# Feed-forward of two superblocks by Strassen's seven products, with the weight-block sums made in the first superblock

## The chip, the cores and the metric

The kernel runs on one core of one Trainium2 chip. Its time is device microseconds of one execution; the figures below are medians over runs. The engines are TensorE (PE, with its weight load PEld), VectorE (DVE), ScalarE (ACT), GpSimd (POOL) and SyncE (SP), whose queue issues all DMA transfers here.

## The reference

One decoder layer for 2048 prompt tokens and 64 sample tokens (8 sequences of 8), model width 1024, all in float32. In order: an RMS norm and one input projection into q, k, v and u; sliding-window attention and a pooling mixer; an output projection; cross-attention into 256 memory tokens; then the feed-forward that this case is about; then a final RMS norm.

```python
    x = x + o @ w_co
    h = _rmsnorm(x, g_ffn)
    x = x + jnp.square(jax.nn.relu(h @ w_up)) @ w_down
```

`w_up` is 1024 by 4096 and `w_down` 4096 by 1024.

## The kernel before

Tokens lie on the free axis, channels on the 128 partitions. The 2112 tokens go through the layer in three superblocks of two blocks each: 384 + 384, 384 + 384, and 256 + 320 (the last block carries the 64 sample tokens). `superblock(s, blks, nxt)` runs the stages of one superblock: input projection mixed with window attention, output projection (`wo`), cross-attention (folded weights `A` and `B`), feed-forward. A residual x of 8 chunks of 128 channels lies in `XT[b]`, one tile for a block.

Every float32 operand of a matmul is held as a rounded part and a remainder (`hi`, `lo`), and each product is three matmuls: hi by hi, hi by lo, lo by hi (`mm3` at L108, `dense` at L267). Weights come as a stream: `Stream.emit` (L125) loads a 128 by 1024 block by DMA into one of six staging buffers `FS`, ACT rounds it into `th` (L132), DVE subtracts into `tl` (L133). There are twelve such buffers `WS`, so six pairs; `Stream.next` (L143) hands out the next pair in a fixed order and `pump` (L137) starts the loads that free buffers allow, at most five ahead. During window attention four of the twelve hold the keys (`kz`).

The feed-forward goes over eight groups of 512 hidden channels. `up(g)` (L1130) takes four weight blocks; for each and for both blocks of tokens it adds 24 matmuls into one PSUM bank, and `up_evac` (L1114) evicts it: ACT relu (L1122), GpSimd square (L1123), ACT rounding (L1125), DVE remainder (L1126). `down(g)` (L1135) takes four weight blocks; each gives two output chunks of 12 matmuls a block, which DVE adds to x (L1156). The order is up(0), up(1), down(0), up(2), down(1) and so on; ahead of down(6) and down(7) `norm1` begins the next superblock's first norm from a fresh load of x. Four PSUM banks (`MM`) rotate here, four more (`AUX`) serve the other stages. `Norm` (L184) squares on ACT, adds on GpSimd (L206), sums over partitions by a matmul with ones (L214) and takes the power by Ln and Exp on ACT; `apply` (L226) scales on DVE (L232), rounds on ACT (L233) and subtracts on DVE and GpSimd in turn (L235). Functions put into `later` run a few steps on, piece by piece, at each `flush` (L301), so that a norm's work stands between the matmuls of other chunks; `order` (L258) puts block 0's last three chunks ahead of block 1's, so that block 0's norm runs while block 1 is still being multiplied. Dependencies and semaphores come from the tile framework, which also sets the order of each engine's queue.

## Time and profile before

| what | value |
|---|---|
| runs | 2638.93, 2640.9, 2646.47 us; median 2640.9 |
| span of the profiled execution, first to last instruction | 2639.7 us (its time as a whole is not given apart) |
| busy PE, PEld | 2565.7 us (97%), 2458.0 us (93%) |
| busy DVE, ACT, POOL | 1302.4 us (49%), 984.2 us (37%), 680.7 us (26%) |
| DMA | 244.76 MB, mean 93 GB/s |
| mean granted TensorE clock | 0.992 |

The busy share is an average over all stages. Matmuls are pipelined, so the duration of one (some 0.33 us at 384 columns) is longer than the distance between the starts of two. An arrow in a row names what ended the idle time ahead of the instruction.

### The profile page before, as it was taken

The numbers are of one execution on the slowest core, as the hardware profiler recorded it, in microseconds if no ns is written. First come the engines' busy times: TensorE is split into PE (matmuls) and PEld (weight loads), VectorE is DVE, ScalarE is ACT, GpSimd is POOL, SyncE is SP. The second block draws the span as 40 slices with busy tenths as digits, with TensorE's granted clock in tenths as the row PEclk, the third lists the DMA queues.
The fourth block names the chain that finished last, engine by engine and source line by source line (L and its number), as shares of the span: only waits on it lengthen the run. The fifth ranks groups of instructions, "written<-read, shape, count | busy, mean of one in ns | idle before, by whom it ended". The sixth has DMA issues, their size and how long they took to land. (4 is left out here: it accounts for less than half of the span.)

```text
span 2639.7 us, 39195 instructions
## 1 busy us (share of the span) xinstructions
PE 2565.7 (97%) x15725; PEld 2458.0 (93%) x15725; DVE 1302.4 (49%) x2276; ACT 984.2 (37%) x1923; POOL 680.7 (26%) x730
## 2 busy tenths in 40 slices
PE   7899999999999999999999999999999999999998
PEld 7798979999999999997999999999999669999998
DVE  7568453633333357936363333334766646334334
ACT  6666342422222244834342222223355434332231
POOL 3215322411111153433241111113334214111111
PEclk9999999999999999999999999999999999999999
DMA  7843212211111123131111111112414473222210
GB/s 261 260 130 101 72 49 74 71 64 63 61 62 64 56 72 113 45 132 56 65 58 63 65 64 64 65 56 71 140 60 149 176 266 112 87 80 81 88 57 37
DMA packets 92251, 244.76 MB, mean 93 GB/s; under 512 B 16740, under 2 KB 31524, under 8 KB 90916
## 3 DMA queue, kind: packets, MB, share of 16 engines
q1 hardware_dynamic: 92068, 242.25, 26.9%
q8 instruction: 123, 2.02, 0.3%
q14 instruction: 60, 0.49, 0.1%
HBM read 219.53 MB, written 22.69 MB: 92 GB/s over the span
## 5 line engine op out<-in xcount | busy, mean ns | idle before, releaser
L281 PE MATMUL mm<-act,w 128*128 128x384 f32 (+2 forms) x2784 | 899.1, 323 | 6.5 <-DVE act L235 5.0
L280 PE MATMUL mm<-act,w 128*128 128x384 f32 (+2 forms) x2784 | 902.8, 324 | 2.5 <-ACT act L623 1.6
L282 PE MATMUL mm<-act,w 128*128 128x384 f32 (+2 forms) x2784 | 897.4, 322 | 1.1 <-DVE w L133 0.9
L132 ACT CAST w<-f 128x1024 fp32r<-128x1024 f32 x330 | 346.9, 1052 | 737.4 <-PE mm L112 453.9
L133 DVE TENSOR_TENSOR w<-f,w 128x1024 fp32r<-128x1024 f32 x330 | 422.8, 1286 | 317.9 <-ACT w L132 312.0
L111 PE MATMUL mm<-act,w 128*128 128x384 f32 (+2 forms) x1728 | 554.1, 321 | 13.6 <-ACT act L372 8.3
L112 PE MATMUL mm<-act,w 128*128 128x384 f32 (+2 forms) x1728 | 550.3, 318 | 0.0
L113 PE MATMUL mm<-act,w 128*128 128x384 f32 (+2 forms) x1728 | 549.8, 318 | 0.0
L281 PEld LDWEIGHTS mm<-act,w 128*128 128x128 f32 x2784 | 527.3, 189 | 16.3 <-DVE act L235 6.7
L280 PEld LDWEIGHTS mm<-act,w 128*128 128x128 f32 x2784 | 527.4, 189 | 7.2 <-issue 2.3
L282 PEld LDWEIGHTS mm<-act,w 128*128 128x128 f32 x2784 | 527.3, 189 | 1.8 <-DVE w L133 1.6
L1123 POOL TENSOR_TENSOR t<-t 128x384 f32<-128x384 f32 (+2 forms) x192 | 219.0, 1141 | 1034.8 <-ACT t L1122 1034.8
L1156 DVE TENSOR_TENSOR x<-mm,x 128x384 f32<-128x384 f32 (+2 forms) x384 | 199.7, 523 | 326.5 <-PE mm L113 326.5
L111 PEld LDWEIGHTS mm<-act,w 128*128 128x128 f32 x1728 | 328.6, 190 | 15.8 <-ACT act L372 8.3
L112 PEld LDWEIGHTS mm<-act,w 128*128 128x128 f32 x1728 | 328.3, 190 | 1.2 <-DVE act L373 0.2
L113 PEld LDWEIGHTS mm<-act,w 128*128 128x128 f32 x1728 | 328.4, 190 | 0.1
L206 POOL TENSOR_TENSOR t<-t,t 128x384 f32<-128x384 f32 (+2 forms) x168 | 203.0, 1209 | 348.9 <-ACT t L205 331.4
L1126 DVE TENSOR_TENSOR act<-t,act 128x384 fp32r<-128x384 f32 (+2 forms) x192 | 103.2, 537 | 300.4 <-ACT act L1125 300.4
L1125 ACT CAST act<-t 128x384 fp32r<-128x384 f32 (+2 forms) x192 | 93.8, 488 | 237.5 <-POOL t L1123 237.5
L1122 ACT ACTIVATE t<-mm 128x384 f32<-128x384 f32 (+2 forms) x192 | 88.2, 459 | 95.2 <-PE mm L282 94.2
L205 ACT ACTIVATE t<-x 128x384 f32<-128x384 f32 (+2 forms) x140 | 68.4, 499 | 145.4 <-DVE x L1085 64.9
L111 PE MATMUL mm<-w,act 128*128 128x512 f32 x288 | 116.7, 406 | 3.2 <-ACT f L330 1.7
(184 smaller groups left out, 2199.0 us busy)
## 6 DMA issues: line engine op xcount, KB each, us to landing
f<-in_wup SPq DMA_DIRECT2D x96, 512.0 KB, 3.5
f<-in_wdn SPq DMA_DIRECT2D x96, 512.0 KB, 3.5
f<-in_win SPq DMA_DIRECT2D x30, 512.0 KB, 3.6
f<-a_s SPq DMA_DIRECT2D x24, 512.0 KB, 3.2
f<-b_s SPq DMA_DIRECT2D x24, 512.0 KB, 4.2
x<-in_x SPq DMA_DIRECT2D x6, 1536.0 KB, 7.1
f<-in_wco SPq DMA_DIRECT2D x16, 512.0 KB, 4.9
f<-in_cmk SPq DMA_DIRECT2D x16, 512.0 KB, 4.5
```

The lines of the kernel that those rows point to most:

```text
L111: nc.tensor.matmul(ps, Wh(k), Hh(k), start=first and i == 0, stop=False)
L112: nc.tensor.matmul(ps, Wh(k), Hl(k), start=False, stop=False)
L113: nc.tensor.matmul(ps, Wl(k), Hh(k), start=False, stop=final and i == last)
L132: nc.scalar.copy(th[:], r[:, 0:1024])
L133: eng.tensor_tensor(tl[:], r[:, 0:1024], f32(th[:]), ALU.subtract)
L206: nc.gpsimd.tensor_tensor(self.acc[:, 0:n], self.acc[:, 0:n], t[:, 0:n], ALU.add)
L280: nc.tensor.matmul(ps[:, 0:n], w8(th)[:, k, :], hi(b, k), start=k == 0, stop=False)
L281: nc.tensor.matmul(ps[:, 0:n], w8(th)[:, k, :], lo(b, k), start=False, stop=False)
L282: nc.tensor.matmul(ps[:, 0:n], w8(tl)[:, k, :], hi(b, k), start=False, stop=k == 7)
L1123: nc.gpsimd.tensor_tensor(q[:, 0:n], r[:, 0:n], r[:, 0:n], ALU.mult)
L1126: nc.vector.tensor_tensor(lo, q[:, 0:n], f32(hi), ALU.subtract)
L1156: nc.vector.tensor_tensor(bl.x(m), ps[:, 0:n], bl.x(m), ALU.add)
```

## The change

The feed-forward of superblocks two and three is written anew; the first keeps the plain form.

- Tokens are cut into two halves of 384 or 288 (`nh`), and channels and hidden channels into two parts, which makes 2 by 2 blocks. `ups(g)` does seven products of 4 contraction chunks for two pairs of hidden chunks; `uevac` puts the outputs together from PSUM, applies relu and square on ACT and keeps the hidden values in float32 in `FB`. `downs(g)` does seven products of 2 contraction chunks for four pairs of output chunks and adds each into an accumulator: four of the seven live in x's own place, two (`MC`) apart, and product 1 goes into two of them. `merge` combines the six accumulators once, ahead of the last down group, which stays plain.
- The input's sums and their splits are made once (`half_ready`) and kept in 14 of the 16 `ACTS` tiles. The hidden values' sums are made on GpSimd and split for each product (`hsplit`), two products ahead, in the two other tiles.
- The sums of weight blocks are made in the first superblock's feed-forward (`prep_steps`): 60 jobs, one every second eviction step, each of which loads a block, makes five sums on DVE and stores six blocks into DRAM scratch. The plain blocks and a copy of the input projection and of the last down group go there too, copied within DRAM. Each of the seven blocks of a group is then one load of 128 by 1024.
- Weights from DRAM scratch are loaded straight into `tl` and split in place; those from the kernel's inputs still go through `FS`. `WS` has ten buffers instead of twelve, the scratch tiles `TS` six instead of eight; `FS` is cut from two large tiles `FB`, of which the feed-forward takes both; the keys `kz` have a tile of their own.
- x lies by chunk rather than by block: each of the two `XT` tiles holds four chunks for all tokens of the superblock.

```diff
+ST0 = [0, 768, 1536]
+STN = [768, 768, 576]
+WIX = {1: 0, 7: 1, 6: 2, 4: 3, 2: 4, 5: 5, 3: 6}
+ORD = (2, 4, 5, 3, 1, 7, 6)
...
-def tile_hybrid_step_kernel(ctx: ExitStack, tc: tile.TileContext, io, nW=12, nF=6, nT=8):
+def tile_hybrid_step_kernel(ctx: ExitStack, tc: tile.TileContext, io, nW=10, nT=6):
...
-    FS = Slots([sb(f"f{i}", 1088) for i in range(nF)])
+    FB = [sb(f"fb{i}", 3072) for i in range(2)]
+    FH = [[FB[h][:, 1024 * i:1024 * i + 1024] for i in range(3)] for h in range(2)]
+    FS = Slots(FH[1] + FH[0])
+    CP = [sb(f"cp{i}", 512) for i in range(2)]
...
+    win_s = drp.tile([10, P, 1024], F32, name="win_s", tag="win_s")
+    us_s = drp.tile([8, 7, P, 1024], F32, name="us_s", tag="us_s")
+    ds_s = drp.tile([7, 7, P, 1024], F32, name="ds_s", tag="ds_s")
+    dn_s = drp.tile([4, P, 1024], F32, name="dn_s", tag="dn_s")
...
         def emit(self):
-            key, raw, eng = self.items.popleft()
+            key, raw, eng, ext = self.items.popleft()
             th, tl = WS.get(), WS.get()
-            r = FS.get()
+            r = FS.get() if ext else f32(tl[:])
...
             eng.tensor_tensor(tl[:], r[:, 0:1024], f32(th[:]), ALU.subtract)
-            FS.put(r)
+            if ext:
+                FS.put(r)
             self.ready.append((key, th, tl))
...
+                for i in ORD:
+                    if g < 8:
+                        S.add(("us", s, g, i), us_s[g, WIX[i]])
+                for i in ORD:
+                    if 0 < g < 8:
+                        S.add(("ds", s, g - 1, i), ds_s[g - 1, WIX[i]], eng=nc.gpsimd if i in (5, 1) else None)
+                if g == 8:
+                    for c in range(4):
+                        S.add(("dn", s, 7, c), dn_s[c])
...
-        kz = [[WS.get() for _ in range(2)] for _ in range(2)]
+        kzt = mc_tile(F32R)
+        kz = [[kzt[:, 896 * (2 * kv + hl):896 * (2 * kv + hl) + 896] for hl in range(2)] for kv in range(2)]
...
+        def split(i, src):
+            hi, lo = ACTS.get(), ACTS.get()
+            Xc[i] = (hi, lo)
+            for j in range(2):
+                c = slice(2 * nh * j, 2 * nh * j + 2 * nh)
+                nc.scalar.copy(hi[:, c], src[:, c])
+                nc.vector.tensor_tensor(lo[:, c], src[:, c], f32(hi[:, c]), ALU.subtract)
+        def comb(dst, other, op, eng=None):
...
+        def half_ready(h):
+            X11, X21, X12, X22 = hx[0, 0], hx[1, 0], hx[0, 1], hx[1, 1]
+            if h == 0:
+                split(2, X11)
+                yield
+                comb(X21, X11, ALU.subtract)
+                split(4, X21)
+                yield
+            else:
+                split(5, X22)
+                yield
+                comb(X12, X22, ALU.subtract)
+                split(3, X12)
+                yield
+                comb(X11, X22, ALU.add)
+                split(1, X11)
+                yield
+                comb(X21, X11, ALU.add)
+                split(7, X21)
+                yield
+                comb(X12, X11, ALU.add)
+                split(6, X12)
+                yield
+                for j in range(2):
+                    x4 = XT[j][:, 0:4 * T].rearrange("p (a m t) -> p a m t", a=2, m=2)
+                    v = x4[:, :, 1, nh:2 * nh]
+                    nc.gpsimd.tensor_tensor(v, v, x4[:, :, 1, 0:nh], ALU.add)
+                    nc.gpsimd.tensor_tensor(v, v, x4[:, :, 0, nh:2 * nh], ALU.subtract)
...
+            yield
+            if blks[0].n == nh:
+                yield from half_ready(b)
+            elif b == 1:
+                yield from half_ready(0)
+                yield from half_ready(1)
...
+        def uevac(g, i, q, ps):
+            p = ps[:, 0:nh]
+            c11, c12, c21, c22 = R(g, 0, 2 * q), R(g, 1, 2 * q), R(g, 0, 2 * q + 1), R(g, 1, 2 * q + 1)
+            def relu2(v):
+                nc.scalar.activation(v, v, AF.Relu)
+                nc.scalar.activation(v, v, AF.Square)
+            if i in (2, 5):
+                t = hold[i, q] = TS.get()
+                nc.scalar.copy(t[:, 0:nh], p)
+            if i == 4:
+                nc.vector.tensor_tensor(c21, p, hold[2, q][:, 0:nh], ALU.add)
+                hold[4, q] = ps
+                relu2(c21)
+                return
+            if i == 5:
+                p4 = hold.pop((4, q))
+                nc.vector.tensor_tensor(c11, p4[:, 0:nh], hold[5, q][:, 0:nh], ALU.subtract)
+                unbank(p4)
+            if i == 3:
+                t2, t5 = hold.pop((2, q)), hold.pop((5, q))
+                nc.vector.tensor_tensor(c12, p, t5[:, 0:nh], ALU.add)
+                nc.vector.tensor_tensor(c22, p, t2[:, 0:nh], ALU.subtract)
+                TS.put(t2, t5)
+                relu2(c12)
...
+        def ups(g):
+            for i in ORD:
+                th, tl = S.next(("us", s, g, i))
+                while i not in Xc:
+                    flush()
+                Hh, Hl = Xc[i]
+                for q in range(2):
+                    ps = bank()
+                    mm3(ps[:, 0:nh], range(4), lambda k: th[:, 512 * q + P * k:512 * q + P * k + P], lambda k: tl[:, 512 * q + P * k:512 * q + P * k + P],
+                        lambda k: Hh[:, nh * k:nh * k + nh], lambda k: Hl[:, nh * k:nh * k + nh])
+                    uevac(g, i, q, ps)
+                    flush()
+                WS.put(th, tl)
...
+        def macc(i, p):
+            if i in (4, 5):
+                return MC[i - 4][:, p * nh:p * nh + nh]
+            m, h = {7: (0, 0), 3: (0, 1), 2: (1, 0), 6: (1, 1)}[i]
+            return xrow(s, 2 * p + m, h * nh, h * nh + nh)
...
+        def hsplit(g, i, dst):
+            X11, X21, X12, X22 = R(g, 0, 0, 2), R(g, 0, 2, 2), R(g, 1, 0, 2), R(g, 1, 2, 2)
+            pre = {4: (X21, X11, ALU.subtract), 3: (X12, X22, ALU.subtract), 1: (X11, X22, ALU.add),
+                   7: (X21, X11, ALU.add), 6: (X12, X11, ALU.add)}.get(i)
+            if pre:
+                nc.gpsimd.tensor_tensor(pre[0], pre[0], pre[1], pre[2])
+            src = {2: X11, 5: X22, 4: X21, 3: X12, 1: X11, 7: X21, 6: X12}[i]
+            hi, lo = dst[:, 0:2 * nh], dst[:, 2 * nh:4 * nh]
+            nc.scalar.copy(hi, src)
+            nc.vector.tensor_tensor(lo, src, f32(hi), ALU.subtract)
+            return hi, lo
+        def downs(g, after=None):
+            hc = {}
+            LEAD = len(HC)
+            def make(j):
+                if j < 7:
+                    hc[j] = hsplit(g, ORD[j], HC[j % LEAD])
+                if j == 6 and after is not None:
+                    after()
+            for j in range(LEAD):
+                make(j)
+            for j, i in enumerate(ORD):
+                th, tl = S.next(("ds", s, g, i))
+                Hh, Hl = hc[j]
+                for p in range(4):
+                    ps = bank()
+                    mm3(ps[:, 0:nh], range(2), lambda k: th[:, 256 * p + P * k:256 * p + P * k + P], lambda k: tl[:, 256 * p + P * k:256 * p + P * k + P],
+                        lambda k: Hh[:, nh * k:nh * k + nh], lambda k: Hl[:, nh * k:nh * k + nh])
+                    v = ps[:, 0:nh]
+                    if i == 1:
+                        nc.vector.tensor_tensor(macc(7, p), v, macc(7, p), ALU.add)
+                        nc.vector.tensor_tensor(macc(6, p), v, macc(6, p), ALU.add)
+                    elif g == 0 and i in (4, 5):
+                        nc.scalar.copy(macc(i, p), v)
+                    else:
+                        nc.vector.tensor_tensor(macc(i, p), v, macc(i, p), ALU.add)
+                    unbank(ps)
+                    if p % 2:
+                        flush()
+                WS.put(th, tl)
+                make(j + LEAD)
...
+        def merge():
...
+            e0, e1 = (nc.gpsimd, nc.vector) if last else (nc.vector, nc.gpsimd)
+            do(nc.vector, M6, M2, ALU.subtract)
+            do(e0, M7, M4, ALU.add)
+            do(e0, M7, M5, ALU.subtract)
+            do(e0, M2, M4, ALU.add)
+            do(e1, M6, M3, ALU.add)
+            do(e1, M3, M5, ALU.add)
...
+            FS.take(FH[0])
+            FS.take(FH[1])
+            HC = [ACTS.get(), ACTS.get()]
+            ups(0)
+            for g in range(1, 8):
+                ups(g)
+                if g < 7:
+                    downs(g - 1)
+            for i in ORD:
+                ACTS.put(*Xc.pop(i))
+            def free0():
+                FS.add(FH[0])
+                if nxt is not None:
+                    norm1(nxt[0])
+            def hid7():
+                for b in range(2):
+                    hh, hl = hid[(7, b)] = [ACTS.get(), ACTS.get()]
+                    for j in range(2):
+                        c = slice(2 * nh * j, 2 * nh * j + 2 * nh)
+                        r = R(7, b, 2 * j, 2)
+                        nc.scalar.copy(hh[:, c], r)
+                        nc.vector.tensor_tensor(hl[:, c], r, f32(hh[:, c]), ALU.subtract)
+                FS.add(FH[1])
+            downs(6, free0)
+            ACTS.put(*HC)
+            hid7()
+            merge()
+            if nxt is not None:
+                norm1(nxt[1])
+            down(7)
...
+        def load(x):
+            kind, g, j = jobs[x]
+            t = MC[x % 2]
+            if kind == "u":
+                c, o = 4 * g + j // 2 * 2, 256 * (j % 2)
...
+                if j == 0:
+                    nc.sync.dma_start(us_s[g, WIX[3]].rearrange("p (q x) -> q p x", q=2),
+                                      io["wup"][4 * g:4 * g + 4].rearrange("(q m) p x -> q m p x", m=2)[:, 0, :, 0:512])
+                    if g < 5:
+                        nc.sync.dma_start(win_s[2 * g:2 * g + 2], io["win"][2 * g:2 * g + 2])
...
+        def sums(x):
+            t = MC[x % 2]
+            b = [t[:, 256 * i:256 * i + 256] for i in range(6)]
+            for d, a, c, op in ((4, 2, 3, ALU.add), (5, 0, 1, ALU.add), (2, 2, 0, ALU.subtract), (1, 1, 3, ALU.subtract), (0, 0, 3, ALU.add)):
+                nc.vector.tensor_tensor(b[d], b[a], b[c], op)
+        def store(x):
+            kind, g, j = jobs[x]
+            dst = (us_s if kind == "u" else ds_s)[g].rearrange("i p x -> p i x")[:, 0:6, 256 * j:256 * j + 256]
+            nc.sync.dma_start(dst, MC[x % 2][:, 0:1536].rearrange("p (i x) -> p i x", i=6))
+        for x in range(len(jobs) + 2):
+            if x - 2 >= 0:
+                store(x - 2)
+            if x < len(jobs):
+                load(x)
+            if 0 <= x - 1 < len(jobs):
+                sums(x - 1)
+            yield
```

275 lines of the change are left out of this document (195 added, 80 removed).

## The prediction

> **What bounds the kernel now.** I read four views in this order: the busy shares, the busy time by stretch for the three feed-forward stages, the waits of TensorE, and the time line of single instructions inside a stage.
>
> ```profile
> span 2639.7 us, 39195 instructions
> ...
> PE 2565.7 (97%) x15725; PEld 2458.0 (93%) x15725; DVE 1302.4 (49%) x2276; ACT 984.2 (37%) x1923; POOL 680.7 (26%) x730
> ```
>
> ```profile
> core 0: us, PE busy (x) PEld busy (x) DVE busy (x) ACT busy (x) POOL busy (x), PEclk, DMA share, GB/s
> 472.00:1003.00 531.00, 529.06 (x3043) 527.02 (x3042) 215.53 (x298) 153.67 (x250) 121.89 (x106) 1.00 0.20 66
> 1326.00:1860.00 534.00, 530.84 (x3051) 528.51 (x3051) 208.54 (x294) 150.26 (x247) 112.02 (x100) 1.00 0.18 62
> 2212.00:2615.00 403.00, 401.23 (x2981) 399.83 (x2979) 166.21 (x260) 117.33 (x205) 79.92 (x77) 1.00 0.21 71
> ```
>
> ```profile
> PE mm L281 <- DVE act L235: 5.0, 6, 1.3
> ```
>
> The second table has one row for the feed-forward of each superblock. TensorE is busy for all but 2 or 3 us of each, at full clock, while DVE is below 42% and DMA at a fifth. The last row is the norm-to-matmul wait at the starts of dense stages: 5.0 us in six places. So a matmul taken out of a feed-forward stage is worth its full pace, as long as nothing else becomes the bound. The pace by tile width is read from starts of matmuls that lie 24 apart:
>
> ```profile
> 1300.00 0.33 PE L281 MATMUL mm<-act,w 128*128 128x384 f32 x1
> ...
> 1304.16 0.33 PE L281 MATMUL mm<-act,w 128*128 128x384 f32 x1
> ```
>
> ```profile
> 2399.78 0.28 PE L280 MATMUL mm<-act,w 128*128 128x256 f32 x1
> ...
> 2402.66 0.31 PE L280 MATMUL mm<-act,w 128*128 128x320 f32 x1
> ...
> 2406.18 0.28 PE L280 MATMUL mm<-act,w 128*128 128x256 f32 x1
> ```
>
> 384 columns: 4.16/24 = 0.1733 us. 256: 2.88/24 = 0.120 us. 320: 3.52/24 = 0.1467 us. The new halves of superblock three are 288 wide; midway gives 0.1333 us.
>
> **Removed: matmuls.** A feed-forward has 3072 of them (64 up and 64 down chunk-halves of 24). With seven products, an up group takes 7 x 2 x 12 = 168 instead of 192, eight times; a down group takes 7 x 4 x 6 = 168 instead of 192, seven times; the last down group stays. That is 360 fewer in each of two superblocks: 360 x 0.1733 = 62.4 us in the second, 360 x 0.1333 = 48.0 us in the third, 110.4 us together. A pair of one up and one down group falls from 384 matmuls to 336: 66.6 to 58.2 us, and 51.2 to 44.8 us.
>
> **Added: evacuation, splits and sums.** The durations (least, median and most of a line, in ns, over its three widths):
>
> ```profile
> L133 DVE TENSOR_TENSOR w<-f,w x330: 1187/1226/2036, 6.0 to 2586.5; 128x1024 fp32r<-128x1024 f32 x165
> ```
>
> ```profile
> L1156 DVE TENSOR_TENSOR x<-mm,x x384: 414/557/558, 541.0 to 2628.2; 128x384 f32<-128x384 f32 x128, 128x256 f32<-128x256 f32 x32, 128x320 f32<-128x320 f32 x32
> ```
>
> ```profile
> L1126 DVE TENSOR_TENSOR act<-t,act x192: 414/558/1378, 477.9 to 2576.1; 128x384 fp32r<-128x384 f32 x128, 128x256 fp32r<-128x256 f32 x32, 128x320 fp32r<-128x320 f32 x32
> ```
>
> ```profile
> L206 POOL TENSOR_TENSOR t<-t,t x168: 722/1020/2025, 12.7 to 2613.7; 128x384 f32<-128x384 f32 x112, 128x256 f32<-128x256 f32 x28, 128x320 f32<-128x320 f32 x28
> ```
>
> An eviction takes 0.557 us at 384 columns and 0.414 at 256, so 0.45 at 288, a quarter of the way. Between L1126 (384 columns, 0.558) and L133 (1024 columns, 1.226) a SBUF subtract of 768 columns takes 0.96 us, of 576 columns 0.76 us. DVE work per pair: ups 16 evictions and 7 weight splits; downs 32 evictions, 7 activation splits and 5 weight splits (two go to GpSimd). Second superblock: 48 x 0.557 + 12 x 1.226 + 7 x 0.96 = 48.1 us under 58.2 of TensorE. Third: 48 x 0.45 + 14.7 + 5.3 = 41.6 us under 44.8. In both DVE still fits on the average, but it is no longer cover, and it is uneven. In downs, evictions 17.8, five splits in the phase 4.8 (the first two have their inputs early) and six weight splits 7.4 make 30.0 us against 168 x 0.1733 = 29.1; in the third 14.4 + 3.8 + 7.4 = 25.6 against 22.4. Two activation buffers mean that the split for product j+2 starts when product j ends and must be done one product later (4.16 or 3.2 us), so DVE may lag by about 3.1 or 2.3 us before TensorE stops; ups, where DVE needs 18 of 29 and 16 of 22 us, gives the lag back. The surplus of 0.9 us is inside the slack in the second, and 3.2 us less 2.3 leaves 0.9 us a pair in the third. The product that adds into two accumulators (eight evictions) comes just ahead of the last split and pushes the lag up once more, by 2.4 us in either.
>
> All this needs engines whose queues aren't in the order of the program text: there, every weight split would hold the evictions behind it on DVE until its DMA has landed. These rows show that the queue has another order: the four scalings of L232 stand ahead of the first subtract of L235, which the code writes after the first of them, and an eviction stands between.
>
> ```profile
> 462.96 2.21 DVE L232 SCALAR_TENSOR_TENSOR t<-x,vec,t 128x384 f32<-128x384 f32 x4
> 465.09 0.55 DVE L235 TENSOR_TENSOR act<-t,act 128x384 fp32r<-128x384 f32 x1
> 465.55 0.55 DVE L1085 TENSOR_TENSOR x<-mm,x 128x384 f32<-128x384 f32 x1
> ```
>
> So I don't charge a DMA landing at every weight. What I charge is DVE against GpSimd:
>
> ```profile
> 1399.83 1.23 DVE L133 TENSOR_TENSOR w<-f,w 128x1024 fp32r<-128x1024 f32 x1 [2.48 <-ACT w L132]
> ```
>
> ```profile
> 1400.27 1.48 POOL L1123 TENSOR_TENSOR t<-t 128x384 f32<-128x384 f32 x1 [4.05 <-ACT t L1122]
> 1403.71 0.83 POOL L1123 TENSOR_TENSOR t<-t 128x384 f32<-128x384 f32 x1 [1.97 <-ACT t L1122]
> ...
> 2226.64 2.14 POOL L235 TENSOR_TENSOR act<-t,act 128x320 fp32r<-128x320 f32 x2 [0.88 <-ACT act L233]
> ```
>
> ```profile
> 2226.95 1.09 DVE L235 TENSOR_TENSOR act<-t,act 128x320 fp32r<-128x320 f32 x1
> ```
>
> A GpSimd square that starts under a DVE subtract takes 1.48 us, alone 0.83; a DVE subtract that starts under a GpSimd one takes 1.09 us, where L1126 at 256 to 384 columns has 0.41 to 0.56. Evictions from PSUM never grew: no L1156 is above 0.558. Here GpSimd gets five sums and two weight splits a pair: by L206's 1.02 us for 384 columns, 5 x 2.04 + 2 x 2.72 = 15.6 us in the second, 13.1 in the third, of which about half falls into downs. With GpSimd active a third of downs, a wait of 1 us for a third of the eleven SBUF subtracts adds some 3 us a pair. Against the slack: second superblock 0 to 3 us a pair, I take 0.7, times 7 = 5 us; third 0.9 to 6.5, I take 3.1, times 7 = 22 us.
> The Trainium skill, page "SBUF — State Buffer", section "Who interferes with whom", says that VectorE with two SBUF inputs and GpSimd take turns on one port pair, an exclusive lock for a whole instruction, and that the one that starts second blocks fully. The trace agrees (1.48 against 0.83, 1.09 against at most 0.56); the mechanism stands below as the second rival.
>
> **Added: the start of the two stages.** The input must now be complete in both halves, then summed. The start of the third stage today:
>
> ```profile
> 2210.90 0.42 DVE L1085 TENSOR_TENSOR x<-mm,x 128x256 f32<-128x256 f32 x1
> ...
> 2217.01 0.49 DVE L219 SCALAR_TENSOR_TENSOR t<-t 128x320 f32<-128x320 f32 x1
> ...
> 2218.58 1.48 DVE L232 SCALAR_TENSOR_TENSOR t<-x,vec,t 128x320 f32<-128x320 f32 x3
> ```
>
> From the last block's eviction to its first scaling pass 7.7 us, which block 0's chunks cover. In the third superblock block 0 has 256 tokens and a half has 288, so no product can start before block 1 is normalised: 7 us, eight scalings of 288 columns (0.45) and eight of 32 (between 0 and 0.41, taken as 0.2), 5.2 us, and half a split (0.8): 13 us of idle TensorE. Then DVE owes seven splits and five sums in two pieces of 0.76 us (18 us), evictions (7) and weight splits (7), 32 us, to 22.4 of TensorE: 10 more, 23 us in all (15 to 30). In the second superblock half 0 is ready and covers two products (8.3 us), but half 1 needs 7 + 4.5 + 1.9 us, and the last four products wait for 3.84 us of sums and splits beside 2.4 of other DVE work each, against 4.16: 5 + 10 = 15 us (8 to 22).
>
> **Added or moved, smaller.** Ends of the stages: six sums over the accumulators and the split of the last group; the inputs of most are early and four PSUM banks cover 8.3 us; 4 us for both (0 to 12). Ring of ten weight buffers without a staging buffer: the load waits until the buffer's last matmul, then 3.5 us landing, 1.05 cast and 1.23 subtract = 5.8 us:
>
> ```profile
> f<-in_wup SPq DMA_DIRECT2D x96, 512.0 KB, 3.5
> ```
>
> ```profile
> L132 ACT CAST w<-f x330: 1031/1053/1067, 5.0 to 2585.4; 128x1024 fp32r<-128x1024 f32 x165
> ```
>
> Where four pairs are held at once (cross-attention) only one is ahead instead of two: about 4 us at its half and 1.6 at the next stage, partly covered; 8 us over three superblocks (0 to 18). The remaining layout edits (six scratch tiles, x by halves, split buffers for the next x) sit under TensorE's 97%; 0 (-3 to 5).
> First superblock: 60 jobs of five 256-column DVE sums, 60 x 5 x 0.41 = 123 us beside 215.5 in 531, covered. DMA: 60 loads of 0.52 MB, 60 stores of 0.79, 31 copies' worth of 17.3, and 33.5 of weights, 129.5 MB in 531 us = 244 GB/s instead of 66, on SP's queue, where each load waits for a store and the weight loads queue behind it; four pairs ahead are 33 us of cover. From 80 to 130 us the trace moves much, mostly in small packets:
>
> ```profile
> DMA packets 12204, 14.09 MB, mean 282 GB/s; under 512 B 669, under 2 KB 8861, under 8 KB 12200
> ...
> q1 hardware_dynamic: 12200, 14.04, 90.6%
> ```
>
> That is 282/0.906 = 311 GB/s when full; 244 is 78% of it. I charge 3 us (0 to 15).
>
> **Sum.** -110.4 + 15 + 23 + 5 + 22 + 4 + 8 + 3 = -30 us. The profiled span is 2639.7 us, 1.2 below the median of the runs, 2640.9; 2640.9 - 30 = 2611 us.
>
> **Rivals.** (1) It hides: only the smallest start costs stay (8 + 15) and 5 us in the third stage: 110.4 - 28 = 82 us gained, 2558 us. For it: DVE's average load fits. Against: downs alone is above 100% of DVE.
> (2) The shared port turns DVE and GpSimd into one serial resource. If all GpSimd time falls on DVE, a pair takes 48.1 + 15.6 = 63.7 us and 41.6 + 13.1 = 54.7 us, which is 5.5 and 9.9 over TensorE, times 7 = 38 and 69 us instead of my 5 and 22: 80 more, 2691 us. It turns the gain into a loss from 30/80 = 38% of that overlap on. For it: the rows of 1.48 and 1.09; against: evictions, more than half of DVE's work, don't take part, and most sums can run in ups.
> (3) The weight-block sums pace the first stage. It decides when DMA gives less than 129.5 MB/561 us = 231 GB/s; at 215 it takes 602 us, 71 more: 2682 us. Against: 282 GB/s measured; for: copies inside DRAM and the chain load, sum, store.
>
> **Chances.** Forecast 0.50 (its own range 2585 to 2640); rival 1 0.14; rival 2 0.27, in part only; rival 3 0.09. What a measurement can tell from no change is about 0.3%, 8 us. Faster: 0.44 + 0.14 = 0.58. Same, from the upper flank of the forecast and the lower ones of rivals 2 and 3: 0.06 + 0.06 + 0.02 = 0.14. Slower, their rest: 0.21 + 0.07 = 0.28. Range 2558 to 2675: rival 1 at its end, most of rivals 2 and 3, without their full prices.
>
> **What would show it.** 720 fewer feed-forward matmuls at 0.173 and 0.133 us; TensorE idle about 13 us ahead of the third feed-forward; DVE above 85% in the third stage with TensorE waiting for the activation split; the first stage still 531 us at about 240 GB/s. Wrong if downs waits are a few us in total (then 2560 to 2580) or if DVE subtracts of 0.96 us grow past 1.5 us throughout (then above 2641).

## The result, and the profile after

The changed kernel takes 2773.2 us (2771.6 to 2775.4, four runs); the kernel before took 2641.8 us beside it. The ratio is 1.050, 95% interval 1.049 to 1.052: 131 us slower, where I had forecast 30 us faster, and outside my range.

From the page of the changed kernel: span, busy shares with instruction counts, DMA.

```profile
span 2769.8 us, 39420 instructions
...
PE 2535.3 (92%) x15005; PEld 2396.4 (87%) x15005; DVE 1783.0 (64%) x3134; ACT 1185.7 (43%) x2195; POOL 741.6 (27%) x702
...
DMA packets 190606, 387.92 MB, mean 140 GB/s; under 512 B 20512, under 2 KB 119776, under 8 KB 190176
```

TensorE has the 720 matmuls fewer that I counted (15725 to 15005) and is still the bound, but it now stands idle for 234 us of the span instead of 74. Where, is read from the busy time by stretch. The rows are the first feed-forward; the start, middle and end of the second; the start, middle and end of the third.

```profile
core 0: us, PE busy (x) PEld busy (x) DVE busy (x) ACT busy (x) POOL busy (x), PEclk, DMA share, GB/s
534.00:1152.00 618.00, 554.93 (x3045) 546.39 (x3044) 304.24 (x552) 150.37 (x241) 100.61 (x99) 0.94 0.55 182
1505.00:1560.00 55.00, 43.26 (x214) 40.81 (x215) 50.81 (x61) 30.47 (x48) 12.74 (x7) 0.88 0.25 81
1560.00:1920.00 360.00, 359.58 (x2072) 358.86 (x2072) 285.16 (x407) 187.18 (x267) 99.57 (x45) 1.00 0.39 127
1920.00:1980.00 60.00, 49.74 (x273) 48.33 (x271) 53.20 (x72) 27.61 (x45) 24.39 (x16) 0.95 0.44 141
1980.00:2025.00 45.00, 31.38 (x175) 30.55 (x176) 37.01 (x52) 19.49 (x40) 28.45 (x32) 0.84 0.27 92
...
2345.00:2390.00 45.00, 34.46 (x228) 33.50 (x229) 42.77 (x70) 26.19 (x47) 12.17 (x5) 0.80 0.30 95
2390.00:2690.00 300.00, 290.27 (x2110) 285.07 (x2109) 249.29 (x412) 168.07 (x273) 88.65 (x45) 0.99 0.47 155
2690.00:2759.00 69.00, 60.24 (x392) 57.04 (x391) 51.45 (x83) 23.67 (x41) 23.49 (x16) 0.93 0.23 77
```

In the middle of the second feed-forward TensorE is busy for 359.6 of 360 us. The losses lie elsewhere: in the first feed-forward, which computes what it did before, and at both ends of the other two. The next table adds the stages ahead of the first feed-forward, which take 59.5 us more than before.

The stages of five kernels, in us, each from the first eviction of one stage to that of the next (a feed-forward: to its last eviction). e1, e2 and e15 are experiments below.

| stage | before | after | e1: no jobs | e2: buffers alone | e15: no plain copies |
|---|---|---|---|---|---|
| start to first output projection | 270.6 | 291.0 | 287.7 | 286.9 | 281.4 |
| output projection to product B | 133.5 | 159.0 | 146.1 | 145.5 | 149.4 |
| B to feed-forward | 70.3 | 83.9 | 70.7 | 71.9 | 82.0 |
| first feed-forward | 537.7 | 622.7 | 541.8 | 544.0 | 561.5 |
| to second feed-forward | 338.9 | 348.3 | 340.8 | 347.7 | 344.7 |
| second feed-forward | 536.1 | 520.3 | 517.5 | 538.5 | 517.5 |
| to third feed-forward | 326.0 | 334.8 | 335.2 | 322.1 | 334.1 |
| third feed-forward | 415.6 | 399.1 | 398.9 | 415.1 | 397.1 |

What TensorE waits for in the first feed-forward of the changed kernel (total us, times, longest), and what SyncE's queue waits for there:

```profile
PE mm L323 <- ACT w L160: 20.5, 4, 11.4
PE aux L257 <- POOL t L249: 16.4, 4, 8.3
PE mm L141 <- DVE w L161: 14.9, 6, 3.1
```

```profile
SPq L1560 <- DVE mc L1555: 275.6, 47, 46.7
SPq L159 <- DVE w L161: 40.1, 5, 19.8
```

TensorE waits 46 us for weight casts and splits (L160, L161; two shorter rows of theirs, 5.7 and 5.1 us, are left out) and 16 us for the sum of a norm's squares (L249). SyncE, which issues the weight loads (L159), stands for 276 us at the jobs' stores (L1560), until VectorE has made the sums (L1555). One such wait in the time line, SyncE first, then VectorE, ScalarE and TensorE:

```profile
756.43 0.33 SPq L1547 DMA_DIRECT2D mc<-in_wdn  x1
778.33 0.38 SPq L1560 DMA_DIRECT2D ds_s<-mc  x1
778.75 0.54 SPq L159 DMA_DIRECT2D fb<-in_wup  x1
```

```profile
776.07 0.56 DVE L1268 TENSOR_TENSOR act<-t,act 128x384 fp32r<-128x384 f32 x1 [3.60 <-ACT act L1267]
776.54 3.44 DVE L1555 TENSOR_TENSOR mc<-mc 128x256 f32<-128x256 f32 x10
```

```profile
784.27 1.04 ACT L160 CAST w<-fb 128x1024 fp32r<-128x1024 f32 x1 [8.23 <-DMA fb<-in_wup]
```

```profile
785.37 0.69 PE L323 MATMUL mm<-act,w 128*128 128x384 f32 x1 [11.36 <-ACT w L160]
...
788.71 0.53 PE L325 MATMUL mm<-act,w 128*128 128x384 f32 x1
789.03 0.39 PE L323 MATMUL mm<-act,w 128*128 128x384 f32 x1
...
789.61 0.35 PE L323 MATMUL mm<-act,w 128*128 128x384 f32 x1
789.79 0.34 PE L324 MATMUL mm<-act,w 128*128 128x384 f32 x1
```

Read from the end: TensorE idles 11.4 us for a cast; the cast waits 8.2 us for its load; the load was issued at 778.75, right behind a store; the store had stood from 756.8 to 778.3, until the sums of 776.5; and the sums stand in VectorE's queue behind an eviction (776.07), which came when TensorE's product did. It is a ring: TensorE sets when the sums come, and through SyncE's queue the sums set when TensorE's weights come. After the gap the matmuls start some 0.32 us apart for 3.7 us (785.37 to 789.03), and then 0.18 us.

This is the longest wait, and most of the others are a shorter ring that leaves SyncE out. Of the other 35 us for weights, 19 us (eight waits) end with a subtract that stood right behind a job's sums in VectorE's queue, and 9 us (three waits) with a cast that stood right behind an eviction's cast in ScalarE's. One of the eight, whose load landed 7.9 us after its issue, at 973.3 us:

```profile
965.45 0.73 SPq L159 DMA_DIRECT2D fb<-in_wdn  x1
```

```profile
974.06 1.05 ACT L160 CAST w<-fb 128x1024 fp32r<-128x1024 f32 x1
```

```profile
980.94 1.88 DVE L1555 TENSOR_TENSOR mc<-mc 128x256 f32<-128x256 f32 x5
982.74 1.22 DVE L161 TENSOR_TENSOR w<-fb,w 128x1024 fp32r<-128x1024 f32 x1
```

```profile
984.02 0.69 PE L141 MATMUL mm<-act,w 128*128 128x384 f32 x1 [3.06 <-DVE w L161]
```

The block was there in time. Its subtract stood behind the sums, and these behind an eviction that ended at 981.0. Nor does a stand of SyncE cost anything by itself: at 567 us it began to stand 46.7 us at one store, and between 560 and 780 us TensorE waited 1.3 us in all.

### The profile page after: what moved, and what is told of

The parts are those of the page before. It is cut to its first block, busy times and chain, and to the rows that moved or that the text cites. A ratio compares the mean times of both kernels' runs of the same rounds, so it can differ in the third digit from the quotient of the medians.

```text
span 2769.8 us, 39420 instructions
## 1 busy us (share of the span) xinstructions
PE 2535.3 (92%) x15005; PEld 2396.4 (87%) x15005; DVE 1783.0 (64%) x3134; ACT 1185.7 (43%) x2195; POOL 741.6 (27%) x702
## 2 busy tenths in 40 slices
DMA packets 190606, 387.92 MB, mean 140 GB/s; under 512 B 20512, under 2 KB 119776, under 8 KB 190176
## 5 line engine op out<-in xcount | busy, mean ns | idle before, releaser
L323 PE MATMUL mm<-act,w 128*128 128x384 f32 (+2 forms) x1760 | 588.0, 334 | 38.0 <-ACT w L160 29.9
L325 PE MATMUL mm<-act,w 128*128 128x384 f32 (+2 forms) x1760 | 582.4, 331 | 7.9 <-DVE w L161 7.9
L324 PE MATMUL mm<-act,w 128*128 128x384 f32 (+2 forms) x1760 | 582.9, 331 | 3.1 <-DVE act L278 2.0
L139 PE MATMUL mm<-act,w 128*128 128x384 f32 (+2 forms) x1672 | 548.1, 328 | 38.7 <-ACT act L1185 15.2
L140 PE MATMUL mm<-act,w 128*128 128x384 f32 (+2 forms) x1672 | 546.2, 327 | 16.9 <-DVE act L1413 8.7
L141 PE MATMUL mm<-act,w 128*128 128x384 f32 (+2 forms) x1672 | 543.9, 326 | 18.7 <-DVE w L161 18.6
L161 DVE TENSOR_TENSOR w<-w,w 128x1024 fp32r<-128x1024 f32 x274 | 366.8, 1345 | 78.7 <-ACT w L160 77.6
L160 ACT CAST w<-w 128x1024 fp32r<-128x1024 f32 x302 | 314.6, 1047 | 222.5 <-DMA w<-us_s 97.3
L323 PEld LDWEIGHTS mm<-act,w 128*128 128x128 f32 x1760 | 340.6, 194 | 45.5 <-ACT w L160 33.0
L139 PEld LDWEIGHTS mm<-act,w 128*128 128x128 f32 x1672 | 325.8, 195 | 45.0 <-ACT act L1185 17.3
L325 PEld LDWEIGHTS mm<-act,w 128*128 128x128 f32 x1760 | 339.2, 193 | 12.6 <-DVE w L161 11.9
L140 PEld LDWEIGHTS mm<-act,w 128*128 128x128 f32 x1672 | 325.8, 195 | 25.6 <-DVE act L1413 13.1
L324 PEld LDWEIGHTS mm<-act,w 128*128 128x128 f32 x1760 | 339.6, 193 | 9.4 <-DVE act L278 3.1
L141 PEld LDWEIGHTS mm<-act,w 128*128 128x128 f32 x1672 | 326.4, 195 | 22.3 <-DVE w L161 21.4
L249 POOL TENSOR_TENSOR t<-t,t 128x384 f32<-128x384 f32 (+3 forms) x168 | 191.6, 1141 | 399.3 <-ACT t L248 388.4
L139 PE MATMUL aux<-act,w 128*128 128x384 f32 (+1 forms) x840 | 267.3, 318 | 2.6 <-DVE x L1438 2.6
L140 PE MATMUL aux<-act,w 128*128 128x384 f32 (+1 forms) x840 | 267.0, 318 | 0.0
L141 PE MATMUL aux<-act,w 128*128 128x384 f32 (+1 forms) x840 | 266.3, 317 | 0.0
L1409 POOL TENSOR_TENSOR fb<-fb 128x768 f32<-128x768 f32 (+1 forms) x70 | 139.2, 1992 | 340.1 <-DVE act L1413 274.8
L160 ACT CAST w<-fb 128x1024 fp32r<-128x1024 f32 x118 | 123.0, 1049 | 217.2 <-DMA fb<-in_wdn 74.9
L161 DVE TENSOR_TENSOR w<-fb,w 128x1024 fp32r<-128x1024 f32 x118 | 148.7, 1266 | 72.1 <-ACT w L160 71.7
L1265 POOL TENSOR_TENSOR t<-t 128x384 f32<-128x384 f32 x64 | 63.5, 992 | 442.4 <-ACT t L1264 420.8
```

The source lines that it names most:

```text
L139: nc.tensor.matmul(ps, Wh(k), Hh(k), start=first and i == 0, stop=False)
L140: nc.tensor.matmul(ps, Wh(k), Hl(k), start=False, stop=False)
L141: nc.tensor.matmul(ps, Wl(k), Hh(k), start=False, stop=final and i == last)
L160: nc.scalar.copy(th[:], r[:, 0:1024])
L161: eng.tensor_tensor(tl[:], r[:, 0:1024], f32(th[:]), ALU.subtract)
L249: nc.gpsimd.tensor_tensor(self.acc[:, 0:n], self.acc[:, 0:n], t[:, 0:n], ALU.add)
```

## The experiments

**e1 and e2: jobs, buffers and Strassen apart.** e1 keeps Strassen and the buffers and leaves the jobs out; e2 keeps the buffers alone.

```
e1: - work = iter(prep_steps(MC)) if s == 0 else None
    + work = iter(()) if s else copy_win()     # one copy of ten blocks
    - S.add(("us", s, g, i), us_s[g, WIX[i]])
    + S.add(("us", s, g, i), win_s[WIX[i]])    # ds, dn, wo alike
e2: as e1, and up/down of the first superblock (staged loads) in all three
```

> Strassen's products and the new buffers stay; the 60 jobs that make the weight-block sums are left out (no loads, sums, stores or copies of blocks), and superblocks two and three read all their weights from one scratch of ten blocks, so their weights are not the right ones; number, size and place of the weight loads in the stream are the same. Theory A (the jobs are the loss, inside the first feed-forward and ahead of it): the first feed-forward goes back from some 618 to 537-545 us and the stages ahead of it give back 40 or more of their 60 us, 2773 - 75 - 45 = 2653 us, down to 2632 us. Rival B (the smaller ring and the unstaged loads are the loss ahead of the first feed-forward): those 60 us stay, 2692 us or more. Rival C (Strassen's own work holds the time up, jobs only a little): above 2740 us.

> The buffers and the layout of the changed kernel, but the plain feed-forward in all three superblocks and no weight-block sums; superblocks two and three take the weights of the two projections from a scratch copy of the input projection, so these are not the right ones. This is the price of the buffers alone. Theory A: 2641 + 0 to 15 = 2641 to 2656 us, since TensorE's 97% covers ten weight buffers. Rival B: ahead of the first feed-forward +40 to +60 us, some 8 us in each later superblock: 2695 to 2720 us. With e1 it also gives what Strassen's products are worth with ready-made weights: theory A says about 20 us (what the two stages lost in the changed kernel), my prediction's 110 less 47 would say 60.

e1: 2645.4 us, ratio 1.0016 (1.0004 to 1.0027). e2: 2679.0 us, 1.0143 (1.0124 to 1.0161). So, by medians: buffers 2679.0 - 2641.6 = +37 us; Strassen with ready-made weights 2645.4 - 2679.0 = -34 us; jobs 2773.2 - 2645.4 = +128 us. Together +131. Theory A holds for the jobs; for the buffers neither it (0 to 15) nor B (54 and more) has the size. The first feed-forward without jobs, a window of e1:

```profile
504.00:1046.00 542.00, 537.01 (x3085) 534.39 (x3085) 223.05 (x311) 157.26 (x254) 119.37 (x104) 1.00 0.20 66
```

TensorE is idle for 5 us of it, at full clock; in the changed kernel for 63 of 618, at 0.94.

**e3 and e4: where the jobs stand.**

```
e3: + if s == 0 and (g, c, b) == (0, 0, 0):
    +     for i in range(2):                    # both work buffers
    +         nc.gpsimd.tensor_copy(MC[i][:, 511:513], r[:, 0:2])
    +         nc.gpsimd.tensor_copy(MC[i][:, 1023:1025], r[:, 0:2])
e4: in prep_steps: - nc.sync.dma_start   + nc.scalar.dma_start
```

> As the changed kernel, but the first loads of the weight-block jobs wait for the first eviction of the first feed-forward (a two-column write by GpSimd into both work buffers); copies within DRAM may still go earlier. Theory A1 (the jobs that ran ahead of the feed-forward disturb the output projection and the cross-attention): from wo to the feed-forward 20 to 40 us come back (243 us now, 204 before), the first feed-forward stays 618 or takes up to 20 more for the jobs that it now has to do itself: 2740 to 2760 us. Rival B (that loss is the ring of ten buffers and the lack of staging): 243 us stay, 2773 to 2795 us.

> As the changed kernel, but all DMAs of the weight-block jobs (loads, stores, copies) are issued from ScalarE's queue instead of SyncE's. Theory A2 (the weight loads of the first feed-forward stand behind stores that wait for the sums on SyncE's in-order queue): the first feed-forward falls from 618 to 550-575 us, 2705 to 2740 us. Rival D (the time goes into VectorE waiting for the jobs' loads, or into DMA bandwidth): it stays within 15 us of 2773. Rival E: ScalarE now stands at the jobs' stores ahead of casts and relus, slower than 2785 us.

e3: 2787.1 us (1.0553, 1.0532 to 1.0574), 14 more; ahead of the feed-forward only 1 us came back (532.9 against 533.9) and the feed-forward took 637.6. Holding the jobs alone only moves them: A1 falls, though not in favour of the ring, since e1 with the same ring lost 29 us less there. e4: 2760.1 us (1.0450, 1.0429 to 1.0471); by its total this is rival D. But its stages say otherwise: the copies all went out between 1 and 424 us (between 70 and 1091 in the changed kernel) and the first feed-forward began at 600.2 us, while the feed-forward itself took 556.5, with 179 of the 300 sums still made in it, up to 840 us:

```profile
700.00:800.00 100.00, 98.86 (x563) 98.42 (x563) 58.45 (x121) 23.09 (x36) 12.04 (x13) 0.99 0.78 263
```

TensorE at 99% beside 263 GB/s: bandwidth is not what the changed kernel lacked at 182.

**e5: the weight loads on another queue.**

```
- S.add(("up", s, g, c), io["wup"][4 * g + c], ext=True)
+ S.add(("up", s, g, c), io["wup"][4 * g + c], ext=True, q=nc.scalar)   # dn alike, first superblock
```

> As the changed kernel, but the weight loads of the first feed-forward are issued from ScalarE's queue; the weight-block jobs stay on SyncE's queue, with the same loads, sums, stores and copies in the same place. Theory A2 (weight loads stand behind stores and loads of the jobs that wait, on one in-order queue): the first feed-forward falls from 623 to 545-570 us, in all 2700 to 2725 us. Rival D (VectorE standing at the jobs' sums, or DMA bandwidth, holds TensorE up): it stays above 600 us, 2750 us or more.

2964.7 us (1.1231, 1.1213 to 1.1250), against both theories. The first feed-forward did come down, to 529 us, but only because the jobs hardly moved in it (the last section says why); most were made behind it, with TensorE mostly idle:

```profile
545.00:1074.00 529.00, 526.74 (x3036) 525.78 (x3034) 198.25 (x291) 127.66 (x197) 79.33 (x68) 1.00 0.23 75
1074.00:1390.00 316.00, 54.52 (x221) 46.59 (x222) 156.98 (x326) 42.72 (x82) 45.22 (x48) 0.58 0.73 241
```

It shows a second thing: with little else to do, 48 jobs took 300 us (the stores of L1560, 1075.9 to 1376.1), 6.3 us each; by that pace sixty would take some 375 us, an estimate.

**e6, e8, e14: the 37 us of the buffers.**

```
e6:  e2, - S.add(("A", s, hf, kp), a_s[hf, kp])
         + S.add(("A", s, hf, kp), a_s[hf, kp], ext=True)   # B alike
e8:  before, nT=8 -> nT=6
e14: e2, evac: t = TS.get() -> t = CPS.get()                 # from the copy buffers
```

> As e2 (plain feed-forward everywhere, the new buffers, no weight-block sums; two projections of superblocks two and three from scratch blocks that are not theirs), but the cross-attention weights A and B go through the staging buffers again instead of straight into the weight buffer. Theory F (unstaged loads wait for TensorE to release a buffer and then show their landing): of the 12 us that each superblock loses between the output projection and B (146 against 133.5 us in the first, 146 against 134 in the second) 6 to 12 come back in two of them, 2655 to 2668 us. Rival G (ten buffers instead of twelve are what counts, staged or not): 2674 to 2684 us as e2.

> The kernel before, with six scratch tiles TS instead of eight and nothing else. Theory J (a norm's squares wait for a scratch tile that the store of a memory key or value block still holds, and ScalarE's queue with them): the stages up to the first output projection take 10 to 16 us longer, 2651 to 2657 us. Rival: they are covered as I predicted, 2639 to 2645 us.

> As e2 (plain feed-forward, new buffers, no jobs; two projections from scratch blocks that are not theirs), but the stores of the memory keys and values go from the attention's copy buffers, so that they hold no scratch tile. Theory J2 (in e2 TensorE idled 12 us at 80 to 97 us because ScalarE's squares waited for a scratch tile held by such a store): the first output projection starts 10 to 16 us earlier than in e2 (287 us), 2663 to 2670 us in all. Rival M (with six scratch tiles alone the kernel before lost 1 us there, so it is the order of ScalarE's queue and moves with any edit): it stays within 5 us of 287, 2675 to 2683 us in all.

e6: 2674.0 us (1.0134, 1.0119 to 1.0150). From output projection to B 139.8 and 139.7 us instead of 145.5 and 145.8, so unstaged loads are half of that loss; a little went elsewhere, 5 us in all. e8: 2646.2 us (1.0022, 1.0013 to 1.0032), but not where theory J had it: up to the output projection +1.4, in the first feed-forward +6.1, which is all that e2 lost there (544.0 against 537.7). e14: 2676.3 us (1.0129, 1.0114 to 1.0145); the output projection starts at 282.6 instead of 286.9. J2 falls for the most part. In e9 and e12 that stage takes 274.4 and 270.0 us with the new buffers, and e9 has no edit there. So the 16 us seem to hang on the order that each program's queues get; that is argued, not shown.

**e7 and e10: the end of the second feed-forward.**

```
e7:  norm1(nxt[0]) -> norm1(nxt[0], 6);  norm1(nxt[1]) -> norm1(nxt[1], 5)
e10: nm = Norm(n, lambda k: fb[...], on_pe=bl.s == 2)
```

> As the changed kernel, but at the end of superblock two's feed-forward the next superblock's first norms may finish later: their sums over partitions come six and five steps after the squares are issued instead of two. Theory H (TensorE stands at that sum's matmul, which is queued ahead of the last down group while GpSimd still adds the squares, 16 to 20 us): the second feed-forward falls from 520 to 500-508 us, 2753 to 2763 us in all. Rival I (then the merge of the accumulators or the late norm itself ends the wait, at the start of the next superblock): within 5 us of 2773.

> As the changed kernel, but the sum over the squares of the third superblock's first norms, which falls into the end of the second feed-forward, is made by eight accumulating matmuls with ones on TensorE for each norm instead of seven GpSimd additions and one matmul. Theory H2 (GpSimd's additions, slowed by VectorE's merge, end the 16 to 20 us wait of TensorE at 1990): the second feed-forward falls from 520 to 500-510 us, 2753 to 2763 us in all. Rival I2 (the merge itself and the squares on ScalarE end it): within 5 us of 2773.

e7: 2771.4 us (1.0501, 1.0486 to 1.0517), nothing; the second feed-forward 521.8. The long wait is still there: asking later in the text moved the matmul of one norm back, but that of the other stands where it stood in TensorE's queue, 96 matmul records ahead of the next such sum in both traces. The waits from 1960 to 2000 us, first in the changed kernel, then in e7:

```profile
PE aux L257 <- POOL t L249: 19.6, 2, 16.2
```

```profile
PE aux L257 <- POOL t L249: 15.5, 1, 15.5
```

e10: 2766.1 us (1.0476, 1.0461 to 1.0492); the feed-forward falls by 8 us, to 512.2. H2 has the mechanism and half of the size.

**e9, e11, e12, e13: the order tied by hand.** In e9 each step's instructions are queued behind what the program has already issued on the same engine; no wait is added.

```
e9:  - next(work, None)
     + with tc.issue_after(S.dma), tc.issue_after(beat[1]):   # last weight load, last eviction
     +     next(work, None)
e11: e9 + e10 + e6's staging + e14's edit + merge on VectorE, and in the jobs
     - DRAM copies of the plain blocks   + a store of seven blocks instead of six
e12: e11, prep() also in B's evictions, copies of wo and dn later
e13: e11 without anything of the jobs (weights as in e1)
```

> As the changed kernel with the same work on the same queues; only the order of two queues is tied: each step of the weight-block jobs (loads, sums, stores, copies) is queued on SyncE behind the last weight load, and on VectorE behind the last eviction, that the program has issued ahead of that step. No wait is added or taken away. Theory A3 (it is the order in SyncE's queue: weight loads stand behind stores and loads of jobs that run ahead of their place): the first feed-forward falls from 623 to 545-575 us, and the stages ahead of it give back 10 to 25 of the 29 us that the jobs cost there: 2680 to 2720 us. Rival D (VectorE's waits for the jobs' loads, or DMA bandwidth): the first feed-forward stays above 605 us, 2750 us or more.

> The paced jobs of e9 and the norm on TensorE of e10, and four further edits: the stores of a job write the seventh, plain block too, so that the fifteen copies of plain blocks within DRAM fall away; A and B are staged as in e6; the stores of the memory keys and values go from the attention's copy buffers instead of the scratch tiles; the whole merge of the second superblock is on VectorE. From e1 (2645 us without any jobs): less 5 for staging, 10 for the norm, 0 to 12 for the scratch tiles, plus 10 to 30 for the jobs: 2630 to 2665 us. If pacing does not help the jobs: above 2730 us.

> As e11, but the jobs begin in the stage ahead of the first feed-forward (product B) and so end ahead of the next superblock's first norm; the copies of the output projection and of the last down group come later. Theory K (in e11 the first feed-forward ran at 97% up to 1000 us, and then some 45 us went into a ring of queues: the load of x for that norm behind a job's store on SyncE, the store behind sums on VectorE, those behind an eviction that needs ScalarE's cast, the cast behind the squares of x): the first feed-forward falls from 614 to 555-575 us, 2640 to 2662 us in all. Rival L (the jobs' chain cannot go faster than the steps and the wait only moves): above 2685 us.

> The floor for e12: the edits of e11 that don't concern the jobs (norm on TensorE, A and B staged, memory stores from the copy buffers, merge on VectorE), no jobs at all, weights of superblocks two and three from a scratch of ten blocks that are not theirs. Against e1 (2645 us) I expect 8 for the norm and merge, 5 for staging, and 0 to 15 at the start: 2617 to 2635 us. e12 less this one is the price of the jobs once their order is right.

e9: 2772.9 us (1.0494, 1.0472 to 1.0516). Ahead of the feed-forward 26.5 us came back (507.4), the feed-forward lost them again (649.6). A3 falls in this form. e11: 2703.2 us (1.0243, 1.0218 to 1.0268). Its first feed-forward, 614.5 us, falls into two parts:

```profile
560.00:1000.00 440.00, 426.25 (x2416) 423.45 (x2415) 220.14 (x423) 98.97 (x151) 50.68 (x52) 0.98 0.65 224
1000.00:1095.00 95.00, 63.35 (x315) 58.94 (x314) 64.65 (x109) 28.77 (x54) 35.43 (x29) 0.85 0.62 207
```

Up to 1000 us TensorE is at 97% beside the jobs. Then the ring of the expectation of e12 closes: SyncE stands 68.5 us at one store, with the load of x for the next norm behind it, and ScalarE stands at the squares of that x, with the casts behind them:

```profile
SPq L1559 <- DVE mc L1554: 98.7, 9, 68.5
```

```profile
ACT t L248 <- DMA fb<-in_x: 44.3, 2, 41.7
```

e12 lets the jobs end ahead of that load: 2673.0 us (1.0121, 1.0103 to 1.0139), 100 us faster than the changed kernel; the first feed-forward 582.7. Theory K has the direction, the size was optimistic by 10 us. e13: 2637.0 us (0.9977, 0.9967 to 0.9988). So 2673.0 - 2637.0 = 36 us of jobs are left of 128. But e11 and e12 had two edits to the jobs, the tie and the dropped copies, and e9, with the tie alone, had won nothing.

**e15 and e16: the two edits apart.**

```
e15: changed kernel, in prep_steps
     - nc.sync.dma_start(us_s[g, WIX[3]]..., io["wup"]...)      # ds_s alike: 15 copies
     + dst = (us_s if kind == "u" else ds_s)[g]...[:, :, 256 * j:256 * j + 256]   # store of 7 blocks
e16: e12, - with tc.issue_after(S.dma), tc.issue_after(beat[1]): next(work, None)
          + next(work, None)
```

> The changed kernel with one edit of e11 alone: a job's store writes the plain block too, so that the fifteen copies of plain blocks within DRAM fall away; the order of the queues isn't tied. Theory N (the order is the loss, the copies only a small part): 2750 to 2773 us. Rival O (the copies, in rows of 1 and 2 KB, hold the queue up): 2680 to 2720 us, most of the 92 us that e12 won back on the jobs.

> e12 with the tie of the queue order taken out and all else kept, the early beginning of the jobs in the program and the dropped copies too. Theory N: the jobs run ahead of their place again and the weights of the first feed-forward stand behind them, 2720 to 2760 us. Rival O (dropped copies and the other edits are what made e12 faster): within 15 us of 2673.

e15: 2681.1 us (1.0155, 1.0138 to 1.0171). One edit, 92 us, of which 61 lie in the first feed-forward and 21 ahead of it; rival O is right and my theory N wrong. e16: 2689.6 us (1.0182, 1.0165 to 1.0199): the tie is worth 17 us in e12, not more. It isn't the bytes or the packets: e15 moves 387.91 MB in 192609 packets, the changed kernel 387.92 in 190606. What changed is when the sums are made. The sums alone (VectorE busy, instructions) by fifths, from 285 us on and through the first feed-forward, first the changed kernel, then e15:

```profile
285.00:534.00 249.00, 16.03 (x34) 0.93 0.32 105
534.00:689.00 155.00, 20.64 (x50) 1.00 0.46 151
689.00:843.00 154.00, 25.08 (x65) 0.94 0.46 155
843.00:998.00 155.00, 28.97 (x76) 0.93 0.62 207
998.00:1152.00 154.00, 31.26 (x70) 0.90 0.65 215
```

```profile
285.00:513.00 228.00, 28.61 (x68) 0.96 0.52 177
513.00:653.00 140.00, 38.28 (x95) 1.00 0.78 256
653.00:794.00 141.00, 39.74 (x102) 0.99 0.80 265
794.00:934.00 140.00, 13.81 (x38) 0.99 0.43 141
934.00:1074.00 140.00, 0.00 (x0) 1.00 0.20 68
```

The changed kernel makes sums until its stage ends; e15 has them done by 934 us. The order of VectorE's queue, as the framework wrote it, says the same without any time: ahead of the 32nd of the 64 up evictions stand 105 of the 300 sums in the changed kernel and 219 in e15. That count alone doesn't settle it: in e16 it is 135, SyncE stands 68.2 us at one store, and yet TensorE waits only 2.9 us for weights there and the first feed-forward takes 566.9 us. In e15 the rings open: the sums no longer wait for late evictions, SyncE stands 73 us at stores instead of 276, and no wait for a weight cast or split is left in TensorE's list. SyncE's two longest waits in the first feed-forward of e15, and TensorE's longest:

```profile
SPq L159 <- DVE w L161: 184.9, 39, 10.4
SPq L1556 <- DVE mc L1551: 73.0, 41, 10.2
```

```profile
PE mm L139 <- DVE x L1299: 14.0, 8, 4.1
```

SyncE now stands at the weight loads themselves (L159), until a staging buffer is free: they come early, not late. VectorE's own waits for the jobs' loads (L1555, in e15 L1551) grew there, from 59 to 133 us in all, while the stage became 61 us shorter; so rival D, those waits or bandwidth, isn't what the changed kernel lost by (beside 265 GB/s TensorE was busy for 133 of 141 us). It is what e15 still loses: the 14.0 us are eight evictions that stood behind sums, most of which had waited for their load, the one at 727.48 for 5.75 us.

Why fifteen copies put the sums later isn't shown: the framework may take them for long, or they may delay the job's own transfers. No run that makes the sums beats the kernel before, and e13, which leaves them out, shows why: with jobs that cost nothing and the mended buffers, 0.2% would be left.

## Why the prediction was wrong, step by step

- **Jobs: 3 us (0 to 15) predicted, 128 measured. This is the step that failed.** The sum took VectorE's 123 us of sums as "covered", the weight loads as covered by 33 us ("four pairs ahead"), and the bandwidth as enough. Bandwidth was there (263 GB/s beside 99% in e4). The cover was not: it helps a block whose load, cast and subtract are queued in their place. In the first feed-forward one load stood 21.5 us behind a store that waited for sums, which cost TensorE 11.4 us, and 28 of its 46 us of waits for weights are casts and subtracts that stood behind evictions and sums. I had noted, from VectorE's rows, that queues aren't in the order of the text, and booked it as a help only; I did not ask what it does to a chain of load, sum and store in the queues of the weights. And I had counted the copies as bytes ("31 copies' worth of 17.3"): fifteen of them, 7.9 MB, go with 92 of the 128 us (e15). Of the 36 us that are left (2681.1 - 2645.4), 19.7 lie in the first feed-forward and 11.3 just ahead of it.
- Rival 3 named the right stage, but by bandwidth, with 231 GB/s as its threshold; the stage was held at 182 GB/s and 55% DMA share. What it had noted in favour, the copies within DRAM and the chain of load, sum and store, is what e15 and the traces bear out; that its 71 us for the stage come near the measured 81 (622.7 - 541.8) is luck.
- **Buffers: 8 for the ring plus 0 for the rest, 37 measured.** "Under TensorE's 97%" was no argument: six scratch tiles cost 6 us in the first feed-forward (e8), unstaged loads half of 12 us a superblock in cross-attention (e6). The rest, with 16 us ahead of the first output projection, stays open.
- **Matmuls: right in number; in pace, 360/2072 = 0.1737 us in the second stage (0.1733 predicted), but 300/2110 = 0.142 in the third (0.133).** So the steady loss is none in the second (5 predicted) and 300 - 2110 x 0.1333 = 19 us in the third (22 predicted), where VectorE is at 83%. Rival 2 did not happen: VectorE and GpSimd together did not become the bound in the steady stretch. (Its 1.09 us subtract was set against 0.56, the median of L1126; the most in that row is 1.378.)
- **Starts: 15 and 23 predicted.** 55 - 214 x 0.1733 = 18 us in the second; 45 - 228 x 0.1333 = 15 in the third, nearly all of it the first product, which comes 12.7 us later after B than before (78.3 against 65.6; 13 predicted). The 10 us that VectorE was to owe after that aren't there.
- **Ends: 4 us predicted for both (0 to 12); 105 - 448 x 0.1733 = 27 in the second and 69 - 392 x 0.1333 = 17 in the third.** Missed were the next norm, whose x is loaded only when the hidden buffer is free, and the merge, which I took as hidden by four PSUM banks.
- Starts, steady and ends together are 96 us from these windows, where I had 69; windows with round limits and missing records overstate them. By the runs, Strassen with ready-made weights in these buffers gains 34 us, which leaves 76 us of losses; the same terms of my sum gave 110 - 69 = 41. That total stood in part by luck, since the ends took 44 us instead of 4 and the other terms less than I had charged; what fell was the price of making the weights, and of the room for them.

## What to carry to other kernels

Work that lies "under" an engine's busy share isn't free when its instructions share a queue with the operands of the engine that bounds: follow the ring for each step of the operand, here load, cast and subtract (what stands ahead of it in its queue, what that waits for, and whether this waits for the bound engine in turn). Neither the bytes nor the longest stand of a queue gives the price: 46.7 us at one store cost TensorE next to nothing, 21.5 us at another cost it 11.4. Where a framework writes the queues, a few side transfers can shift the whole chain: try the added work with one of its parts left out. And price the room that a gain needs by itself; one run (e2) would have shown that the buffers take more than Strassen gives.

## What was not expected of the hardware

A gap of 11.4 us on TensorE costs more than itself: the next matmuls of 384 columns start 0.32 us apart instead of 0.18 until 3.7 us later, and the granted clock of the first feed-forward is 0.94 instead of 1.00. The Trainium skill, page "TensorE: Matmul & The Clock Gate", section "Part 1: The HAM clock gate", has the array at half clock after an idle window of about 3.4 us, and at full clock again after as long a busy one; the rows of 785 to 789 us agree. A gap of 3.06 us did it too, and the half pace lasted longer than that rule has it: behind the gap that ends at 824.40 the starts lie 0.32 us apart until 830.01, 5.6 us.

In the merge of the second superblock a sum of 768 columns takes VectorE 0.94 us, and up to 2.59 where GpSimd adds beside it:

```profile
1970.15 2.59 DVE L1459 TENSOR_TENSOR x<-x,mc 128x768 f32<-128x768 f32 x1
1975.53 0.94 DVE L1459 TENSOR_TENSOR x<-x,mc 128x768 f32<-128x768 f32 x1
```

In e5 the jobs' loads on SyncE's queue waited up to 182.4 us for weight loads of ScalarE's queue, whose data they don't use. The trace names what tied them, and it belongs to the program: the transfers of both queues report to the same eight semaphores. The job's load that goes out at 829.41 us waits for semaphore 102, to which the weight load of 826.19 reports too; that one landed at 829.40. So the two queues were not independent chains, but nothing here shows that the chip ties them.

```profile
SPq L1537 <- DMA fb<-in_wup: 230.3, 4, 182.4
```
